# Two-layer decoder with a 32-expert MoE: the last expert pair's rows joined by one-hot products, the loop for crowded experts ahead of that pair

## The chip, the cores and the metric

One Trainium2 chip, and the program runs on one of its cores. The metric is device microseconds of one execution. Instructions run in order on each engine: PE (TensorE), DVE (VectorE), ACT (ScalarE), POOL (GpSimd) and SP (SyncE), which here only issues DMA and evaluates branches. An engine waits on semaphores that other engines or DMA transfers raise.

## The reference

`x` is 512 tokens of 1,024 features, and there are DEPTH = 2 layers, L0 and L1 here. Each layer mixes tokens (three kinds of attention behind one input projection `w_in`), takes a first layer norm, then a mixture of 32 experts with two experts per token, and a second layer norm:

```python
for l in range(DEPTH):
    mix = hybrid_mixer(x, tabs, w_in[l], ...)
    x = layer_norm(DEEPNORM_ALPHA * x + mix, ln1_g[l], ln1_b[l])
    moe = hier_moe(x, ...)
    x = layer_norm(DEEPNORM_ALPHA * x + moe, ln2_g[l], ln2_b[l])
return x
# in hier_moe: gate is zero but for the two experts of each token
h = jax.nn.silu(einsum('td,edf->tef', t, w_gate[g])) * einsum('td,edf->tef', t, w_up[g])
y = y + einsum('tef,efd->td', h * gate[:, g, :, None], w_down[g])
```

All values are float32.

## The kernel before, in words

**Expert stage.** An expert gets room for 64 token rows. Two experts fill the two halves of PE's array and make a *pair*; `p` runs over 16 pairs, pair 15 being the last. For a pair, GpSimd gathers its 128 rows from DRAM (`gathered`, L996), PE turns them (`turned`, L1007), `experts_up` multiplies by gate and up weights (32 products `S<-w,xg`), `experts_mid` takes SiLU (ACT L1040) and the product (DVE L1041), and `experts_down` transposes (PE L297), copies `hT` (ACT L90 and DVE L92 by turns) and multiplies by the down weights (16 products `o<-w,hT`). Two DVE instructions (L1055) scale the result and add it to the row's own share, in a row room of the tile `xroom`. A GpSimd DMA (L1056) then *scatter-adds* the 128 rows into the DRAM tensor `y2`, by the token index `ri`. So the sum over a token's experts is made in DRAM.

`load_next` (L530) issues the expert weights on SP's queue, as rooms of a ring come free. The last pair's weights are cut into smaller transfers.

**Crowded experts.** `overflow()` handles experts with more than 64 rows. Their number of extra *pieces* (`n_items`) is read from the chip's own counts, and a `tc.For_i` loop runs over them: each loads one expert's weights (two transfers, L1152), makes a list of rows, gathers them (L996), computes, and scatter-adds (L1218). With this data there are no pieces in L0 and one in L1: 33 gathers L996, 32 scatters L1056 and one scatter L1218 are in the profile. Where the loop is skipped or left, all engines meet: the branch on SP waits for every DMA queue lane used (DMASW0 to 7 are GpSimd's, DMAHW0 to 7 those of SP) and for the engines' sequencers.

**Second norm.** After the loop, `y2` is read back (L1263) as four tiles of 128 tokens (`yts`, the first in two halves). For each tile: statistics (DVE `bn_stats` L1272, `bn_aggr` L234), a power on POOL (L236), and scale and shift on DVE (L1275, L1277). In L1 the tile goes to the output. In L0 it is kept in DRAM (`res_dram`) and turned by PE (L1287, eight 128x128 transposes per tile), and each result is split into a rounded part `hi` (ACT, L210) and the rest `lo` (DVE, L213) of the next layer's input `xh`.

**Next projection.** The input projection of L1 (`acc<-U,xh`, and the same into banks `S` and `o`) multiplies `xh` by weight chunks: chunk 0 is 328 columns wide, the others 384. A chunk takes 24 products per token tile. Each weight chunk is loaded in four quarters (`load_pair`, L194), each with one cast for `hi` on ACT (L196) and one subtraction for `lo` (L199), on DVE and POOL by turns ("VG"). `warm(10)` issues ten products on constants behind the loop in L0.

`tc.issue_after(x)` places the following instructions behind `x` in its engine's program order; otherwise a scheduler orders instructions ahead of time.

Of the kernel before, what the change touches and what calls it, by code (L numbers as in the profile page):

```python
# [7 lines left out]
F32 = mybir.dt.float32  # L8
# [4 lines left out]
OP = mybir.AluOpType  # L13
# [51 lines left out]
def trunk(tc, a, out, dbg=None):  # L65
# [4 lines left out]
    with es:  # L70
# [9 lines left out]
        def bank(tag):  # L80
            return ps.tile([128, 512], F32, name=tag, tag=tag)
# [166 lines left out]
        for l in range(DEPTH):  # L248
# [739 lines left out]
            def row_room():  # L988
                turns["y"] += 1
                return carve(xroom, UNIT + 2 * D + D * (turns["y"] % 3), [D])  # L990
# [25 lines left out]
            def half_rows(xr, n=128):  # L1016

                y = row_room()
                V.tensor_tensor(y[0:n], xr[0:n], gb1[0:n, 0], OP.mult)
                V.tensor_tensor(y[0:n], y[0:n], gb1[0:n, 1], OP.add)  # L1020
                return y

            def next_half(p1):
                if p1 in XR:
                    with tc.issue_after(last_on["h"].ins):
                        HR[p1] = half_rows(XR.pop(p1))
                    fetch(p1 + 2)

            halves_ = ((0, 64), (64, 128))
# [13 lines left out]

            def experts_down(h, w, rows, y, p1):
                hT = cp.tile([128, 2, 128], F32, name="hT", tag="rw")
                transposes(hT.rearrange("p a b -> p (a b)"), [h[:, 0:128], h[:, 128:256]], 128)
                next_half(p1)
                o = [bank("o") for _ in range(2)]
                for f in range(2):
                    for n in range(2):  # L1050
                        for j, (c0, c1) in enumerate(halves_):
                            last_on["PE"] = mm(o[n][c0:c1], hT[:, f, c0:c1], down(w[j], f, n), f == 0, f == 1)
                for n in range(2):
                    c = slice(512 * n, 512 * n + 512)
                    last_on["V"] = V.scalar_tensor_tensor(y[:, c], o[n], rows[1], y[:, c], op0=OP.mult, op1=OP.add)  # L1055
                return G.indirect_dma_start(out=y2, out_offset=bass.IndirectOffsetOnAxis(ap=rows[0], axis=0), in_=y,  # L1056
                                            in_offset=None, bounds_check=S - 1, oob_is_err=False, compute_op=OP.add)

# [9 lines left out]
            def lists(b, P=None):  # L1068

                Pf = (P or hots(b)).rearrange("p t e s -> p t (e s)")  # L1070
                for q in range(2):
                    t = bank("T")
                    e0 = 4 * b + 2 * q
                    for i in range(NT):
                        mm(t[:, 0:6], Pf[:, i, 128 * q:128 * q + 128], tok[:, i, :, e0:e0 + 2], i == 0, i == NT - 1)
                    rv = small.tile([128, 3], F32, name="rv", tag="rv", bufs=8)
                    V.tensor_copy(rv[0:64], t[0:64, 0:6:2])
                    V.tensor_copy(rv[64:128], t[64:128, 1:6:2])
                    RI[2 * b + q] = slot_rows(rv)

            def fetch(p):
                if p < NE // 2:
# [62 lines left out]
            def overflow():  # L1145

                n_items = nc.values_load(eidi[0:1, MAX_ITEMS:MAX_ITEMS + 1], min_val=0, max_val=MAX_ITEMS)
                with tc.For_i(0, n_items) as item:
# [63 lines left out]
                    for f in range(2):  # L1212
                        for h, c in enumerate(two):
# [4 lines left out]
                    G.indirect_dma_start(out=y2, out_offset=bass.IndirectOffsetOnAxis(ap=ri[0:64], axis=0), in_=y[0:64], in_offset=None,  # L1218
                                         bounds_check=S - 1, oob_is_err=False, compute_op=OP.add)

            for p in range(NE // 2):
                w = (EW.pop(2 * p), EW.pop(2 * p + 1))
                gu = experts_up(XG.pop(p), w)
                load_next()
                h = experts_mid(gu)
                if p + 1 < NE // 2:
                    with tc.issue_after(last_on["up"].ins):
                        XG[p + 1] = turned(XR[p + 1])
                if p % 2 == 0 and p // 2 + 2 < NE // 4:
                    lists(p // 2 + 2)  # L1230
                st = experts_down(h, w, RI.pop(p), HR.pop(p), p + 1)
                load_next()
                if p % 2:
                    tc.declare_no_dep(st.ins, st0.ins, reason="a token has one group: the two pairs of a batch share no row")
                st0 = st
                if p == 3:
                    pieces()

            last = l == DEPTH - 1
            yus = [unit("A", "yt") for _ in range(2)]  # L1240
            gb2 = [yu[:, 2 * D:3 * D] for yu in yus]
            for j in range(2):
                SP.dma_start(gb2[j], a["ln_rows"][l:l + 1, 1, j].to_broadcast([128, D]))
# [12 lines left out]
            yts = []  # L1256
            for j in range(2):
                yu = carve(yus[j], 0, [2, D])
                for i in range(2):
                    yts.append(yu[:, i])  # L1260
                    r = 256 * j + 128 * i
                    for c in halves if r == 0 else [slice(0, 1024)]:
                        y2d = SP.dma_start(yu[:, i, c], y2[r:r + 128, c])  # L1263
            if not last:
                with tc.issue_after(y2d.ins):
                    Wc[l + 1, 1] = load_pair(w_in_src(l + 1, 1), chunks[1][1], "VG")
            for i in range(NT):
                z = yts[i]
                src = [z[:, c] for c in halves]
                st = small.tile([128, 2, 6], F32, name="bst", tag="bst", bufs=4)  # L1270
                for h in range(2):
                    V.bn_stats(st[:, h], src[h])  # L1272
# [10 lines left out]
                for h in range(2):  # L1283
                    t = bank("T")
                    for j in range(4):
                        k = 4 * h + j
                        PE.transpose(t[:, 128 * j:128 * j + 128], z[:, 128 * k:128 * k + 128], ident)  # L1287
                    split(*(XH[l + 1][:, r, 4 * h:4 * h + 4, 128 * i:128 * i + 128] for r in range(2)),
                          t.rearrange("p (k n) -> p k n", k=4))
            moe.__exit__(None, None, None)  # L1290


# [62 lines left out]
```

## Time and profile before

| | us |
|---|---|
| median of 3 runs | 1366.55 (1362.19, 1366.55, 1367.04) |
| profiled execution | 1363.18 |
| its span, first to last instruction | 1361.4 |
| PE busy | 1183.1 (87%) |
| DVE busy | 776.5 (57%) |
| ACT busy | 425.6 (31%) |
| POOL busy | 299.1 (22%) |
| mean granted TensorE clock | 0.953 of full speed |
| DMA | 293.82 MB, 216 GB/s over the span |

Times in the rows are microseconds from the span's start. The expert stages take about the stretches 500 to 645 (L0) and 1160 to 1335 (L1) of it. The profiled execution is 3.4 us (0.25%) under the median of the runs.

### The profile page before, as it was taken

How to read it: one execution, taken by the hardware profiler on the slowest of the kernel's cores; microseconds unless marked ns; L12 is line 12 of the kernel's file. 1: busy time of each engine (PE TensorE's matmuls, PEld its weight loads, DVE VectorE, ACT ScalarE, POOL GpSimd, SP SyncE). 2: the span in 40 equal slices, each digit the busy share in tenths (PEclk: the TensorE clock that was granted, in tenths of full speed). 3: DMA queues.
4: the chain of work that ended last, by engine and by line, in shares of the span. 5: the costliest groups of instructions: out<-in, count | busy, mean ns of one | idle time of the engine just before them, and what ended most of it. 6: DMA issues, size and time to landing. Idle time of an engine off the chain costs nothing. (4 is left out here: it accounts for less than half of the span.)

```text
span 1361.4 us, 18270 instructions
## 1 busy us (share of the span) xinstructions
PE 1183.1 (87%) x6708; PEld 822.5 (60%) x6708; DVE 776.5 (57%) x1905; ACT 425.6 (31%) x1019; POOL 299.1 (22%) x288
## 2 busy tenths in 40 slices
PE   6989999999969997778599899999998799887850
PEld 6989986668944443333398899666797343333320
DVE  6599638674455654323668992667636465433435
ACT  3362257574111111110236322857711111111100
POOL 5332431300011211110342434230010122111101
PEclk9999999999979999999799999899999899998975
DMA  6341340005298999998552424200336899999943
GB/s 233 116 147 57 124 170 12 28 10 216 77 377 330 406 406 411 412 382 298 186 160 77 133 75 140 98 24 23 138 126 246 316 395 408 407 409 409 349 178 125
DMA packets 65115, 293.82 MB, mean 216 GB/s; under 512 B 16000, under 2 KB 20608, under 8 KB 49664
## 3 DMA queue, kind: packets, MB, share of 16 engines
q1 hardware_dynamic: 54496, 271.63, 51.9%
q0 software_dynamic: 9376, 16.81, 5.1%
q10 hardware_dynamic: 1152, 4.19, 0.8%
q8 instruction: 54, 0.88, 0.2%
q14 instruction: 37, 0.30, 0.1%
HBM read 278.06 MB, written 31.82 MB: 228 GB/s over the span
## 5 line engine op out<-in xcount | busy, mean ns | idle before, releaser
L97 PE MATMUL acc<-U,xh 128*128 128x384 f32 (+1 forms) x1584 | 294.8, 339 | 20.5 <-DVE xh L212 7.2
L97 PE MATMUL S<-w,xg 128*64 128x512 f32 (+1 forms) x968 | 270.4, 607 | 45.2 <-DMA w<-w_e 31.2
L97 PEld LDWEIGHTS acc<-U,xh 128*128 128x128 f32 x1584 | 275.3, 190 | 24.6 <-ACT U L196 7.2
L97 PEld LDWEIGHTS S<-w,xg 128*64 128x64 f32 x968 | 91.5, 141 | 171.2 <-issue 100.3
L97 PE MATMUL o<-w,hT 128*64 128x512 f32 x488 | 134.2, 615 | 7.5 <-ACT hT L90 3.9
L1040 ACT ACTIVATE h<-S 128x256 f32<-128x256 f32 x32 | 12.3, 384 | 377.7 <-PE S L97 377.7
L199 POOL TENSOR_TENSOR U<-raw,U 128x768 fp32r<-128x768 f32 (+2 forms) x46 | 90.5, 1972 | 164.5 <-ACT U L196 164.4
L1041 DVE TENSOR_TENSOR h<-h,S 128x256 f32<-128x256 f32 x32 | 13.5, 421 | 189.4 <-ACT h L1040 189.4
L996 POOL DMA_INDIRECT xroom<-xd,ri x33 | 40.6, 1230 | 275.6 <-issue 142.7
L196 ACT ACTIVATE U<-raw 128x768 fp32r<-128x768 f32 (+2 forms) x88 | 68.1, 812 | 85.7 <-PE acc L97 42.1
L1056 POOL DMA_INDIRECT y<-xroom,ri x32 | 51.0, 1595 | 177.2 <-DVE xroom L1055 158.9
L97 PEld LDWEIGHTS o<-w,hT 128*64 128x64 f32 x488 | 43.6, 140 | 73.9 <-issue 51.0
L1055 DVE SCALAR_TENSOR_TENSOR xroom<-o,rv,xroom 128x512 f32<-128x512 f32 x64 | 48.0, 750 | 56.3 <-PE o L97 52.3
L199 DVE TENSOR_TENSOR U<-raw,U 128x768 fp32r<-128x768 f32 (+2 forms) x42 | 51.9, 1238 | 39.5 <-ACT U L196 36.9
L1011 ACT ACTIVATE xg<-acc,lv 128x128 f32<-128x128 f32 x128 | 48.2, 456 | 58.7 <-PE acc L1007 57.5
L90 ACT ACTIVATE uc<-T 128x512 f32<-128x512 f32 (+3 forms) x117 | 51.5, 461 | 40.8 <-PE T L297 39.0
L97 PE MATMUL acc<-U,oh 128*128 128x384 f32 (+1 forms) x384 | 63.3, 315 | 0.0
L97 PEld LDWEIGHTS acc<-U,oh 128*128 128x128 f32 x384 | 56.8, 189 | 1.3 <-issue 1.0
L1007 PEld LDWEIGHTS acc<-cst,xroom 128*128 128x128 f32 x256 | 30.5, 152 | 41.9 <-issue 27.4
L403 DVE MATCH_REPLACE8 uc<-m,uc 128x256 f32<-128x256 f32 (+2 forms) x96 | 51.3, 539 | 0.0
L1013 DVE TENSOR_SCALAR xg<-acc,lv 128x128 f32<-128x128 f32 x128 | 43.6, 402 | 13.5 <-PE acc L1007 13.4
L1007 PE MATMUL acc<-cst,xroom 128*128 128x128 f32 x256 | 38.6, 299 | 14.3 <-DMA xroom<-xd,ri 14.3
(366 smaller groups left out, 1991.7 us busy)
## 6 DMA issues: line engine op xcount, KB each, us to landing
w<-w_e SPq DMA_DIRECT2D x110, 1536.0 KB, 30.7
raw<-w_in SPq DMA_DIRECT2D x64, 384.0 KB, 3.6
xroom<-w_e SPq DMA_DIRECT2D x8, 1536.0 KB, 28.3
w<-w_e SPq DMA_DIRECT2D x24, 512.0 KB, 17.3
raw<-w_o SPq DMA_DIRECT2D x16, 384.0 KB, 3.6
y<-uc SPq DMA_DIRECT2D x2, 2048.0 KB, 7.8
xd<-yn ACTq DMA_DIRECT2D x8, 512.0 KB, 6.8
xroom<-w_e SPq DMA_DIRECT2D x4, 768.0 KB, 14.6
```

Of the source, the lines that this page charges most:

```text
L90: A.activation(o, i, AF.Copy, scale=1.0 if scale is None else scale)
L97: return PE.matmul(o, l, r, start=start, stop=stop, skip_group_check=True)
L196: A.activation(hi, r, AF.Copy)
L199: e.tensor_tensor(lo, r, hi.bitcast(F32), OP.subtract)
L403: V.match_replace(out=acc_t[i][:, :n], in_to_replace=m8, in_values=acc_t[i][:, :n], imm_value=TAKEN)
L996: G.indirect_dma_start(out=xr[0:n], out_offset=None, in_=xd, in_offset=bass.IndirectOffsetOnAxis(ap=ri[0:n], axis=0), bounds_check=S - 1, ...
L1007: PE.transpose(t[:, 128 * j:128 * j + 128], xr[:, 128 * k:128 * k + 128], ident)
L1011: A.activation(xg[:, k], o, AF.Identity, scale=lv[:, 0, k, 0:1], bias=lv[:, 0, k, 1:2])
L1013: V.tensor_scalar(xg[:, k], o, lv[:, 0, k, 0:1], lv[:, 0, k, 1:2], op0=OP.mult, op1=OP.add)
L1041: last_on["h"] = V.tensor_tensor(h, h, gu[:, FH:2 * FH], OP.mult)
L1055: last_on["V"] = V.scalar_tensor_tensor(y[:, c], o[n], rows[1], y[:, c], op0=OP.mult, op1=OP.add)
L1056: return G.indirect_dma_start(out=y2, out_offset=bass.IndirectOffsetOnAxis(ap=rows[0], axis=0), in_=y, in_offset=None, bounds_check=S - 1, ...
```

## The change

Five things are changed.

1. In the last pair, the 128 rows stay in an SBUF tile `y_last` and aren't scattered. `pT`, four transposes of that pair's one-hot lists, turns slots back into tokens: eight products `pT`^T x `y_last` (two 512-wide halves for each of the four tiles) give each token tile's share in PSUM. In L0 DVE adds it to the tile read back (L1295, eight additions). In L1 PE also multiplies the tile read back by the identity into the same PSUM bank, and the norm reads PSUM.
2. A new function `sums()`, called at pair 15 ahead of its `experts_up`, holds `overflow()` and then the loads of `ln_rows` and of the four `y2` tiles, the first no longer in two halves.
3. Chunk 0 of the next projection is loaded within the last `experts_down`, with all four `lo` subtractions on DVE ("V"). Chunk 1 is loaded after the norm of tile 0.
4. `hT` is always copied on DVE.
5. `warm(10)` is left out.

```diff
@@ experts_down
-                transposes(hT.rearrange("p a b -> p (a b)"), [h[:, 0:128], h[:, 128:256]], 128)
+                transposes(hT.rearrange("p a b -> p (a b)"), [h[:, 0:128], h[:, 128:256]], 128, None, "V")
                 next_half(p1)
+                if w_next:
+                    w_next.pop()()
...
+                return y
+
+            def added(y, rows):
                 return G.indirect_dma_start(out=y2, out_offset=bass.IndirectOffsetOnAxis(ap=rows[0], axis=0), in_=y,
                                             in_offset=None, bounds_check=S - 1, oob_is_err=False, compute_op=OP.add)
...
+            def next_weights():
+                with tc.issue_after(last_on["h"].ins):
+                    Wc[l + 1, 0] = load_pair(w_in_src(l + 1, 0), chunks[0][1], "V")
+
+            def sums():
+
+                overflow()
+                yus = [unit("A", "yt") for _ in range(2)]
+                for j in range(2):
+                    SP.dma_start(yus[j][:, 2 * D:3 * D], a["ln_rows"][l:l + 1, 1, j].to_broadcast([128, D]))
+                for j in range(2):
+                    yu = carve(yus[j], 0, [2, D])
+                    for i in range(2):
+                        yts.append(yu[:, i])
+                        r = 256 * j + 128 * i
+                        y2d = SP.dma_start(yu[:, i], y2[r:r + 128, :])
+                return [yu[:, 2 * D:3 * D] for yu in yus], y2d
+
             for p in range(NE // 2):
                 w = (EW.pop(2 * p), EW.pop(2 * p + 1))
+                if p == PL:
+                    gb2, y2d = sums()
                 gu = experts_up(XG.pop(p), w)
...
+                y = experts_down(h, w, rows, HR.pop(p), p + 1)
                 load_next()
...
+                if p < PL:
+                    st = added(y, rows)
...
-            with tc.issue_after(last_on["PE"].ins), tc.issue_after(last_on["V"].ins), tc.issue_after(st.ins):
-                if not last:
-                    raw_room()
-                    Wc[l + 1, 0] = load_pair(w_in_src(l + 1, 0), chunks[0][1], "VG")
-            overflow()
...
-                warm(10)
...
+            for i in range(NT):
+                zb[i] = [bank(("acc", "S", "o")[i % 3]) for _ in halves]
+                for t, c in zip(zb[i], halves):
+                    if last:
+                        mm(t, ident, yts[i][:, c], True, False)
+                    mm(t, pT[:, i], y_last[:, c], not last, True)
             for i in range(NT):
                 z = yts[i]
-                src = [z[:, c] for c in halves]
+                src = [z[:, c] for c in halves] if not last else zb[i]
+                if not last:
+                    for t, c in zip(zb[i], halves):
+                        V.tensor_tensor(z[:, c], z[:, c], t, OP.add)
```

**SP's queue, end of L0's expert stage.** L530 are expert weights, L1243 the norm's `ln_rows`, L194 quarters of chunk 0, and L1147 to L1148 the loop's branch; the last row is where all engines meet. Before:

```order
L530 DMA w<-w_e 128x1024 [waits DMAHW3_49]
L1243 DMA yt<-ln_rows 128x1024 [waits DMAHW4_49,PE_49]
L1243 DMA yt<-ln_rows 128x1024 [waits DMAHW5_49,PE_49]
L194 DMA raw<-w_in 128x656 [waits DMAHW6_49,PE_49]
L194 DMA raw<-w_in 128x656 [waits DMAHW7_49]
L194 DMA raw<-w_in 128x656 [waits DMAHW0_49]
L194 DMA raw<-w_in 128x656 [waits DMAHW1_49]
L1147 TENSOR_LOAD eidi [waits DVE_49]
L1148 COMPARE_AND_BRANCH
L1148 UNCONDITIONAL_BRANCH [waits SP_sequencer_49,DMAHW2_49,DMAHW3_49]
L1148 UNCONDITIONAL_BRANCH [waits DMASW4_49,DMASW3_49,DMASW5_49,DMASW2_49,DMASW6_49,DMASW1_49,DMASW7_49,DMASW0_49,DMAHW0_49,SP_sequencer_49,DMAHW1_49,DVE_sequencer_49,DMAHW2_49,PE_sequencer_49,DMAHW3_49,Activation_sequencer_49,DMAHW4_49
```

The same place in the change (the branch is L1153 to L1154 there):

```order
L530 DMA w<-w_e 128x1024 [waits DMAHW0_49]
L530 DMA w<-w_e 128x1024 [waits DMAHW1_49]
L530 DMA w<-w_e 128x1024 [waits DMAHW2_49]
L530 DMA w<-w_e 128x1024 [waits DMAHW3_49]
L1153 TENSOR_LOAD eidi [waits DVE_49]
L1154 COMPARE_AND_BRANCH
L1154 UNCONDITIONAL_BRANCH [waits SP_sequencer_49,DMAHW4_49,DMAHW5_49]
L1154 UNCONDITIONAL_BRANCH [waits DMASW4_49,DMASW3_49,DMASW5_49,DMASW2_49,DMASW6_49,DMASW1_49,DMASW7_49,DMASW0_49,DMAHW0_49,SP_sequencer_49,DMAHW1_49,DVE_sequencer_49,DMAHW2_49,PE_sequencer_49,DMAHW3_49,Activation_sequencer_49,DMAHW4_49
L1380 BRANCH_PREFETCH_HINT
```

The meeting place now follows the last expert weights directly, and `ln_rows`, the `y2` reads and chunk 0 stand behind it. On PE the 48 products of pair 15 stand behind it too.

**PE, L0, behind the expert stage.** One piece of the difference: transposes of the norm's tiles (L1287 before, L1313 now) and products of the next projection (`U,xh`), whose banks are `acc` for tile 0, `o` for tile 1, `S` for tile 2 and `acc` again for tile 3. The last rows are tile 3's last four transposes of the change. Behind them it has 21 and 24 products left of tile 1's chunks 0 and 1; before, tile 3's last four transposes have only the last 8 products of tile 1's chunk 1 behind them. Then follow tile 2's 48 and tile 3's 48 in both.

```order
+L1313 MATMUL T<-cst,yt 128x128 x16
 L97 MATMUL acc<-U,xh 128x328 x24
-L97 MATMUL acc<-U,xh 128x384 x18
-L1287 MATMUL T<-cst,yt 128x128 x8
-L97 MATMUL acc<-U,xh 128x384 x6
+L97 MATMUL acc<-U,xh 128x384 x3
+L1313 MATMUL T<-cst,yt 128x128 x8
+L97 MATMUL acc<-U,xh 128x384 x21
+L97 MATMUL o<-U,xh 128x328
+L1313 MATMUL T<-cst,yt 128x128 x4
+L97 MATMUL o<-U,xh 128x328 x2
+L1313 MATMUL T<-cst,yt 128x128 x4
```

The transposes of the later tiles have moved ahead of most products of the tiles before them.

**DVE, L0, from the last pair into the norm of tile 0.** L92 copies `hT`, L199 are the `lo` subtractions (656 wide: chunk 0, 768 wide: chunk 1), L1057 is the scale-and-add of the last pair. In the change:

```order
L92 COPY hT<-T 128x256
L199 TENSOR_TENSOR U<-raw,U 128x656
L1057 SCALAR_TENSOR_TENSOR y_last<-o,rv,y_last 128x512
L199 TENSOR_TENSOR U<-raw,U 128x656 x2
L1057 SCALAR_TENSOR_TENSOR y_last<-o,rv,y_last 128x512
L199 TENSOR_TENSOR U<-raw,U 128x656
L1295 TENSOR_TENSOR yt<-yt,acc 128x512
L199 TENSOR_TENSOR U<-raw,U 128x768
L1295 TENSOR_TENSOR yt<-yt,acc 128x512
L1298 BN_STATS bst<-yt 128x6 x2
L199 TENSOR_TENSOR U<-raw,U 128x768
L234 BN_AGGR mv<-bst 128x2
```

Before, two of chunk 0's four subtractions are POOL's, and one stands between the meeting place and the first statistics; in the change all four, and one of chunk 1, stand ahead of the statistics.

## Rows read from the trace of the kernel before

**Rows 1.** Windows: window, length, PE, PEld, DVE, ACT, POOL, clock, DMA share, GB/s.

```profile
1240.00:1270.00 30.00, 26.13 (x106) 8.96 (x106) 8.66 (x14) 2.61 (x8) 4.98 (x4) 0.94 0.99 392
656.50:668.00 11.50, 6.89 (x20) 3.41 (x20) 8.35 (x14) 2.26 (x4) 4.99 (x4) 0.50 0.88 320
740.00:800.00 60.00, 56.53 (x324) 54.79 (x323) 57.00 (x143) 24.07 (x55) 19.85 (x22) 0.97 0.31 96
```

**Rows 2.** Timeline of L0's end, all engines: start, us, instruction, [idle before <-releaser].

```profile
633.86 1.55 POOL L1056 DMA_INDIRECT y<-xroom,ri  x1 [11.10 <-DVE xroom L1055]
...
648.62 1.55 POOL L1056 DMA_INDIRECT y<-xroom,ri  x1 [13.21 <-DVE xroom L1055]
...
649.66 0.84 DVE L199 TENSOR_TENSOR U<-raw,U 128x656 fp32r<-128x656 f32 x1 [1.50 <-ACT U L196]
...
656.34 1.39 ACT L196 ACTIVATE U<-raw 128x656 fp32r<-128x656 f32 x2 [6.03 <-DMA y<-xroom,ri]
...
656.76 4.45 PE L97 MATMUL o<-bfc 128*128 128x512 bf16 x10 [9.39 <-DVE ctr L1143]
...
659.66 0.69 DVE L1272 BATCH_NORM_STATS2 bst<-yt 128x6 f32<-128x512 f32 x1 [0.63 <-DMA yt<-y]
```

**Rows 3.** Timeline of SP's queue, end of L0.

```profile
631.64 0.33 SPq L530 DMA_DIRECT2D w<-w_e  x1
...
656.89 2.46 SPq L1263 DMA_DIRECT2D yt<-y  x5
```

**Rows 4.** DMA issues in 631:633, 633:636, 648:650: size, us to landing.

```profile
w<-w_e SPq DMA_DIRECT2D x1, 512.0 KB, 13.7
...
y<-xroom,ri POOLq DMA_INDIRECT x1, 8.7
...
y<-xroom,ri POOLq DMA_INDIRECT x1, 6.8
```

**Rows 5.** Timeline, the expert pairs: early in L1, then its last ones.

```profile
1065.55 8.40 PE L97 MATMUL S<-w,xg 128*64 128x512 f32 x32
...
1278.02 7.08 PE L97 MATMUL S<-w,xg 128*64 128x512 f32 x30
...
1290.51 1.61 DVE L1055 SCALAR_TENSOR_TENSOR xroom<-o,rv,xroom 128x512 f32<-128x512 f32 x2 [0.53 <-PE o L97]
```

**Rows 6.** DVE groups by shape, 656 to 692: busy, mean ns | idle before.

```profile
L213 DVE TENSOR_TENSOR xh<-T,xh 128x512 fp32r<-128x512 f32 x8 | 5.3, 688 | 0.2 <-ACT xh L210 0.2
L1272 DVE BATCH_NORM_STATS2 bst<-yt 128x6 f32<-128x512 f32 x8 | 5.3, 674 | 2.1 <-DMA yt<-y 2.1
L199 DVE TENSOR_TENSOR U<-raw,U 128x768 fp32r<-128x768 f32 x2 | 2.9, 1453 | 0.0
```

**Rows 7.** Timeline, L0: first transposes, last norm, last transposes, last tile's products.

```profile
665.56 1.97 PE L1287 MATMUL T<-cst,yt 128*128 128x128 f32 x8 [4.36 <-DVE yt L1277]
...
686.41 1.41 DVE L1277 SCALAR_TENSOR_TENSOR yt<-yt,mv 128x512 f32<-128x512 f32 x2
...
687.96 0.63 PE L1287 MATMUL T<-cst,yt 128*128 128x128 f32 x4
...
689.82 7.94 PE L97 MATMUL S<-U,xh 128*128 128x328 f32 x48
```

**Rows 8.** Timeline of L1's loop and second norm.

```profile
1297.20 0.96 SPq L1152 DMA_DIRECT2D w<-w_e  x2
...
1306.90 0.23 DVE L1155 TENSOR_SCALAR h<-cst,ctr 128x16 f32<-128x16 f32 x1
...
1312.38 1.00 POOL L996 DMA_INDIRECT xroom<-xd,ri  x1 [3.72 <-DVE ri L982]
...
1319.14 6.17 PE L97 MATMUL S<-w,xg 128*64 128x256 f32 x32 [2.51 <-DVE xg L1198]
...
1330.74 1.44 POOL L1218 DMA_INDIRECT y<-xroom,ri  x1 [17.35 <-DVE xroom L1217]
...
1335.04 2.51 SPq L1263 DMA_DIRECT2D yt<-y  x5
...
1340.38 0.69 DVE L1272 BATCH_NORM_STATS2 bst<-yt 128x6 f32<-128x512 f32 x1 [1.33 <-DMA yt<-y]
```

**Rows 9.** Last lines of two source views: weights L1152, gathers L996.

```profile
DMA to landing us min/median/max: 13.1/15.2/17.3
...
DMA to landing us min/median/max: 3.1/9.7/12.9
```

More of the change, by code (lines that the diff above doesn't have):

```diff
@@ L1014, in turned, with half_rows @@
                 return xg
-            def half_rows(xr, n=128):
-                y = row_room()
+            def half_rows(xr, n=128, y=None):
+                y = row_room() if y is None else y
                 V.tensor_tensor(y[0:n], xr[0:n], gb1[0:n, 0], OP.mult)
@@ L1025, in next_half @@
                     with tc.issue_after(last_on["h"].ins):
-                        HR[p1] = half_rows(XR.pop(p1))
+                        HR[p1] = half_rows(XR.pop(p1), y=y_last if p1 == NE // 2 - 1 else None)
                     fetch(p1 + 2)
@@ L1079, in lists @@
                     RI[2 * b + q] = slot_rows(rv)
+                return Pf
             def fetch(p):
@@ L1219, in overflow @@
                                          bounds_check=S - 1, oob_is_err=False, compute_op=OP.add)
+            last, PL, w_next, yts = l == DEPTH - 1, NE // 2 - 1, [], []
+            pT = mo.tile([128, NT, 128], F32, name="pT", tag="pT")
+            y_last = mo.tile([128, D], F32, name="y_last", tag="y_last")
+            def next_weights():
[13 more added lines that the diff above has]
+                return [yu[:, 2 * D:3 * D] for yu in yus], y2d
             for p in range(NE // 2):
                 w = (EW.pop(2 * p), EW.pop(2 * p + 1))
+                if p == PL:
+                    gb2, y2d = sums()
                 gu = experts_up(XG.pop(p), w)
@@ L1225, in trunk @@
                 h = experts_mid(gu)
-                if p + 1 < NE // 2:
+                if p < PL:
                     with tc.issue_after(last_on["up"].ins):
                         XG[p + 1] = turned(XR[p + 1])
+                elif not last:
+                    raw_room()
+                    w_next.append(next_weights)
                 if p % 2 == 0 and p // 2 + 2 < NE // 4:
-                    lists(p // 2 + 2)
-                st = experts_down(h, w, RI.pop(p), HR.pop(p), p + 1)
-                load_next()
-                if p % 2:
-                    tc.declare_no_dep(st.ins, st0.ins, reason="a token has one group: the two pairs of a batch share no row")
-                st0 = st
+                    Pf = lists(p // 2 + 2)
+                    if p // 2 + 2 == NE // 4 - 1:
+                        transposes(pT.rearrange("p a b -> p (a b)"), [Pf[:, i, 128:256].bitcast(F32) for i in range(NT)], 128)
+                rows = RI.pop(p)
+                y = experts_down(h, w, rows, HR.pop(p), p + 1)
+                load_next()
+                if p < PL:
+                    st = added(y, rows)
+                    if p % 2:
+                        tc.declare_no_dep(st.ins, st0.ins, reason="a token has one group: the two pairs of a batch share no row")
+                    st0 = st
                 if p == 3:
                     pieces()
[L1239 to L1243, printed above, removed]
-            with tc.issue_after(last_on["PE"].ins), tc.issue_after(last_on["V"].ins), tc.issue_after(st.ins):
-                if not last:
-                    raw_room()
-                    Wc[l + 1, 0] = load_pair(w_in_src(l + 1, 0), chunks[0][1], "VG")
-            overflow()
             if not last:
-                warm(10)
                 XH[l + 1] = xhp.tile([128, 2, NK, S], F32R, name="xh", tag="xh")
@@ L1255, in trunk @@
             halves = [slice(0, 512), slice(512, 1024)]
[L1256 to L1266, printed above, removed]
+            zb = {}
+            for i in range(NT):
[4 more added lines that the diff above has]
+                    mm(t, pT[:, i], y_last[:, c], not last, True)
             for i in range(NT):
                 z = yts[i]
-                src = [z[:, c] for c in halves]
+                src = [z[:, c] for c in halves] if not last else zb[i]
+                if not last:
+                    for t, c in zip(zb[i], halves):
+                        V.tensor_tensor(z[:, c], z[:, c], t, OP.add)
                 st = small.tile([128, 2, 6], F32, name="bst", tag="bst", bufs=4)
@@ L1289, in trunk @@
                           t.rearrange("p (k n) -> p k n", k=4))
+                if i == 0:
+                    with tc.issue_after(y2d.ins):
+                        Wc[l + 1, 1] = load_pair(w_in_src(l + 1, 1), chunks[1][1], "VG")
             moe.__exit__(None, None, None)
```

## Prediction

> **What bounds the kernel now.** I read the windows first, to see what each stage is short of. Late in an expert stage the DMA engines are busy 0.99 of the time at 392 GB/s, while PE has 26.13 of 30 us and DVE 8.66 [rows 1]: the stage lasts as long as its weights take. In L1's projections and attention PE works 56.53 and DVE 57.00 of 60 us [rows 1]: what comes late there stays late. Between the two lies the stretch that the change rebuilds, so I read its timeline, engine by engine, in both layers.
>
> In L0 the last expert weights are issued at 631.64 [rows 3] and take 13.7 to land [rows 4], so they are there at 645.3. Pair 15 runs while they come in, and its scatter is issued at 648.62 [rows 2]. The scatter takes 6.8 [rows 4], to 655.4, and everything stands until then: ACT idles 6.03 "<-DMA y" [rows 2], and PE comes out of the meeting place at 656.76, 1.3 us after the landing. Then `y2` is read (656.89 [rows 3]), the first statistics start at 659.66 [rows 2], and the norm of tile 3 ends at 686.41 + 1.41 = 687.82 [rows 7].
>
> In L1 pair 14 ends at 1290.51 + 1.61 = 1292.12 [rows 5], pair 15 ends before 1306.90, the one piece runs from 1306.90 to its scatter at 1330.74, `y2` is read from 1335.04, and the statistics of tile 0's second half start at 1340.38 [rows 8].
>
> **The change in L0.** It removes pair 15's scatter and the read behind it from the path: from 648.6 to 659.66, some 11 us. It pays by moving the meeting place ahead of pair 15, and that is where the sum turns.
>
> (a) The branch waits for SP's DMA lanes. Ahead of it stand pair 15's weights, which land at 645.3; pair 14's scatter, 633.86 [rows 2] + 8.7 [rows 4] = 642.6, is earlier. With the 1.3 us seen above, PE starts pair 15 at 646.6. Before, most of pair 15 was done by then; now none is.
>
> (b) A pair takes 1292.12 − 1278.02 = 14.1 us [rows 5]. That row has PE at speed (30 of the 32 products recorded, 7.08). A pair behind an idle stretch needed 8.40 [rows 5]; PE will have idled since pair 14, whose scatter is issued at 633.86 [rows 2], some 13 us, so I add 1.3. The bounds are 0 and 2.6: L1's piece, also after idling, took 6.17 for 32 products of half the width, 2.6 over half of 7.08 [rows 8]. Pair 15 then ends at 662.0.
>
> (c) Of chunk 0's subtractions on DVE, two stand between the last two scale-and-adds (2 x 0.84 [rows 2] = 1.7). One follows, then an addition (0.69 as an L213 of the same shape [rows 6]), one subtraction of chunk 1 (0.98, 0.84 scaled by 768/656), and the other addition: 3.2. The products of `y_last`, 0.47 each as an estimate (two half-width products at 7.08/30), hide behind the subtraction. The first statistics start at 662.0 + 1.7 + 3.2 = 666.9, **7.2 later** than 659.66. If the subtractions fall into waits, as one did at 649.66 [rows 2], 3.5 of it goes; at the 1453 ns that two took beside POOL [rows 6] it is some 2.5 more.
>
> (d) From the first statistics to tile 3's end were 28.2 us. The 2.1 us waiting for `y2` go [rows 6]; of 2.9 for two L199 [rows 6] about 1.0 stays; six more additions cost 4.1: +0.1. So tile 3 is 7.3 late.
>
> (e) PE's order. Behind tile 3's last transposes stood 80 products up to the end of its chunk 0 (8 + 48 + 24); now 117 (21 + 24 + 48 + 24). In 689.82's row 48 take 7.94 [rows 7], 0.165 each, and before, they followed the transposes at 687.96 at once. The 37 that PE could have done while it waited for DVE now come after: **+6.1**. It would be 0 if PE reached that place late anyway.
>
> L0 together: **+13.4**, bounds +2.5 (no clock loss, subtractions hidden, order free) and +17.2.
>
> Without a price: the `hT` copies on DVE and the four transposes of `pT` lie under the weights' transfer [rows 1]; without that cover each is under a microsecond a pair. `ln_rows`, `y2` and chunk 0, now issued behind the meeting place, are about 4.3 MB, 11 us at 392 GB/s [rows 1], and land by 658, under pair 15.
>
> **warm(10).** Its ten products took 4.45 [rows 2], and the clock was 0.50 (1.2 GHz) from 656.5 to 668 all the same [rows 1]; the first eight transposes took 1.97 behind them, against 0.63 for four later [rows 7]. So I price the removal at 0.
> The Trainium skill, page "TensorE: Matmul & The Clock Gate", section "Part 1: The HAM clock gate (the "warmup" mystery)", says that the array is at half clock by default and that sustained work releases it. By that rule pair 15's 48 products, now right ahead of the norm, could do what the ten did not: the first transposes would take 1.3 in place of 1.97, and the sum would be 0.7 lower.
>
> **The change in L1.** Here the piece has to run either way; the order is turned around.
>
> (f) The piece begins at 1292.12, and its gather is issued 5.48 later, as before (1312.38 − 1306.90), at 1297.6. Before, the queues were empty by then and it landed in 3.1, the minimum; the median gather, among streaming weights, takes 9.7 [rows 9], and pair 15's weights are still coming. I take 9.7: 1307.3, and the products 3.7 later (1319.14 less 1312.38 + 3.1), at 1311.0. The piece's weights were issued at 1297.20 [rows 8] and landed 13.1 and 17.3 later [rows 9], the first at 1310.3; without 1 MB of `ln_rows` ahead of them (2.6 us at 392 GB/s), 1307.7. They don't bind.
>
> (g) From products to scatter 11.6, from there to the read 4.3 [rows 8]: pair 15 starts at 1326.9. Add 14.1, 1.3 for the clock, 0.9 for identity products that stand between its own, 0.7 for the first product and the first half's statistics: the second half's start at 1343.9, against 1340.38. **+3.5**. With the gather at 3.1 the weights bind, +0.2; at 12.9, +6.7.
>
> **Sum.** 1363.18 + 13.4 + 3.5 = **1380 us**, bounds 1366 and 1387. The sum stands on the profiled execution, 3.4 us under the median of the runs, a quarter of a per cent.
>
> **Rivals.**
> *A. The meeting place does not hold pair 15* (not slower). If the engines pass the skipped loop in L0 without waiting for the weights, pair 15 ends at 648.6 as now. (c) then makes it 653.5 with its 4.9, 6.2 ahead of 659.66; with (d) and (e) L0 is even, and L1's 3.5 gives 1367; with (e) at 0, 1361. It decides once pair 15 ends some 7 us ahead of (b)'s 662.0: then the sum falls within half a per cent of before. For it: only one branch of a skipped loop is taken. Against it: the branch names all DMASW and DMAHW lanes, and the same branch held ACT 6.03 us for a scatter [rows 2]. Chance 0.16.
> *B. L0's delay is made up in L1's attention.* Then only L1's 3.5 stays: 1367. For it: the norm may not be on the path of what comes later, a loaded DVE. Against it: from 740 to 800 PE lacks 3.5 us of 60, DVE 3.0 [rows 1], so 13 us find no room. Half made up gives 1373. Chance 0.17.
> *C. The forecast*, both layers later. Chance 0.67.
>
> **How the numbers follow.** A difference of 0.5%, 6.8 us, is about what a measurement of this kernel tells from none: 1359.7 to 1373.4. C is slower throughout but for its lowest corner (0.03). Of A, 0.09 is faster, where (e) is free and L1's gather quick, the rest the same. Of B, 0.13 is the same and 0.03 slower; 0.01 faster. So faster 0.10, same 0.23, slower 0.67. The range runs from A's 1361 to C's upper bound of 1387 with the 3.4 us of the median added: 1361 to 1391. C alone would be 1368 to 1391.
>
> **What would show it.** (a): in L0 the first `S<-w,xg` of pair 15 near 646.6, with all engines released together after the last weights; before 640 is rival A. (b): pair 15 some 15.4 long, its first products slower than its later ones. (c): first statistics near 667, no idle DVE ahead of them. (d), (e): tile 3's last transposes near 695, and its chunk 0 done near 715 instead of 701. (f): the piece's gather landing some 10 us after its issue. (g): the second statistics of L1 about 17 us later than now in absolute time. The forecast is wrong if PE starts pair 15 early, if PE is still busy when tile 3's transposes come (no 6.1), or if the stretch behind 740 shows idle time that takes the delay up.

## The result, and the profile after the change

The change makes the kernel slower: 1376.3 us (median of 6 runs, 1372.0 to 1378.3) against 1364.8 before (6 runs, 1361.6 to 1368.3), a ratio of 1.0079 with a 95% interval of 1.0056 to 1.0102. The profiled execution took 1375.41, its span is 1373.6, 12.2 longer than that of before.

Of these 12.2 us, 2.9 don't belong to the change. They arise in the first 128 us of the span, where both kernels issue the same instructions in the same order (ACT's runs 0.3 late at 56 us, 1.5 at 80, 2.9 from 128 on). The other kernels profiled below are 1.4 to 4.2 late there too: the profile of before happened to be a quick one. "Net" below means less a kernel's own lateness there, 2.9 for the change. Net, the change's span is 9.3 longer; the medians differ by 11.5.

The first view is L0's last pair, from the timelines of all engines of the changed kernel:

```profile
623.57 12.63 SPq L530 DMA_DIRECT2D w<-w_e  x7
...
637.03 1.55 POOL L1061 DMA_INDIRECT y<-xroom,ri  x1 [11.51 <-DVEq L1154]
...
650.52 1.11 PE L97 MATMUL S<-xroom,xg 128*64 128x512 f32 x1 [14.60 <-DVE ctr L1149]
...
651.64 2.45 SPq L1246 DMA_DIRECT2D yt<-y  x4
...
654.80 0.59 PE L97 MATMUL S<-xroom,xg 128*64 128x512 f32 x1
...
666.60 0.74 DVE L1057 SCALAR_TENSOR_TENSOR y_last<-o,rv,y_last 128x512 f32<-128x512 f32 x1
...
669.48 0.68 DVE L1295 TENSOR_TENSOR yt<-yt,acc 128x512 f32<-128x512 f32 x1
670.08 1.28 DVE L1298 BATCH_NORM_STATS2 bst<-yt 128x6 f32<-128x512 f32 x2
```

PE stands for 14.60 us and starts pair 15 only when the meeting place opens, 14.3 us after the last weights were issued (636.2), close to the forecast's 13.7 + 1.3. The first statistics come at 670.08 against 659.66 [rows 2], 7.5 later net. The windows show the stand, the slow start (clock 0.53) and, in the last row, the norm:

```profile
636.80:650.50 13.70, 0.00 (x0) 0.00 (x0) 0.04 (x1) 0.00 (x0) 1.68 (x2) 0.66 0.38 109
650.50:655.00 4.50, 4.48 (x12) 1.38 (x14) 0.02 (x1) 0.00 (x0) 0.16 (x1) 0.53 0.70 208
655.00:667.40 12.40, 10.94 (x45) 3.58 (x42) 4.65 (x8) 3.64 (x6) 0.00 (x0) 1.00 0.90 333
...
675.40:699.40 24.00, 14.19 (x73) 13.54 (x73) 21.29 (x42) 5.83 (x8) 3.22 (x6) 0.65 0.41 153
```

In the norm PE works 14.19 of 24 us. Its own timeline shows at what it waits:

```profile
677.49 1.97 PE L1313 MATMUL T<-cst,yt 128*128 128x128 f32 x8 [5.12 <-DVE yt L1303]
687.18 1.94 PE L1313 MATMUL T<-cst,yt 128*128 128x128 f32 x8 [7.72 <-DVE yt L1303]
688.77 5.98 PE L97 MATMUL acc<-U,xh 128*128 128x328 f32 x27
...
700.66 0.60 PE L1313 MATMUL T<-cst,yt 128*128 128x128 f32 x4
...
716.23 8.98 PE L97 MATMUL acc<-U,xh 128*128 128x328 f32 x54
```

Between the transposes of tiles 0 and 1 PE idles 7.72 us. Tile 3's last transposes are 9.8 late net (687.96 in [rows 7]), and its chunk 0 starts at 716.23 against 697.60, 15.7 late net.

L1, pair 14's end (1302.23) to the first norm, from the timelines:

```profile
1302.30 0.23 DVE L1161 TENSOR_SCALAR h<-cst,ctr 128x16 f32<-128x16 f32 x1
...
1307.69 1.00 POOL L996 DMA_INDIRECT xroom<-xd,ri  x1 [3.62 <-DVE ri L982]
...
1315.13 1.22 DVE L1019 TENSOR_TENSOR xroom<-xroom,gb 64x1024 f32<-64x1024 f32 x1 [8.24 <-DMA xroom<-xd,ri]
...
1330.30 1.44 POOL L1224 DMA_INDIRECT y<-xroom,ri  x1 [21.61 <-DVE xroom L1223]
...
1334.97 1.11 PE L97 MATMUL S<-xroom,xg 128*64 128x512 f32 x1 [6.51 <-issue]
...
1354.34 0.70 DVE L1298 BATCH_NORM_STATS2 bst<-acc 128x6 f32<-128x512 f32 x1 [0.16 <-PE acc L97]
```

The piece starts right behind pair 14, its gather takes 7.4 us, pair 15 follows the meeting place at 1334.97. From pair 14's end to these statistics are 52.1 us; before it was 48.3 [rows 5, 8].

### The profile page after: what moved, and what is told of

It reads as the page before. It is cut to its first block, busy times and chain, and to the rows that moved or that the text cites. A ratio compares the mean times of both kernels' runs of the same rounds, so it can differ in the third digit from the quotient of the medians.

```text
span 1373.6 us, 18378 instructions
## 1 busy us (share of the span) xinstructions
PE 1206.6 (88%) x6754; PEld 830.2 (60%) x6754; DVE 789.9 (58%) x1930; ACT 422.4 (31%) x1006; POOL 296.1 (22%) x284
## 4 chain that ended last, share of the span: by engine, by line
PE 51%; DMA 25%; DVE 6%; issue 4%; ACT 2%; POOL 1%; SPq 0%; DVEq 0%; ACTq 0%; POOLq 0%
PE acc L97 23%; DMA w<-w_e 22%; PE S L97 12%; PE o L97 10%; PE T L297 5%; DMA xroom<-xd,ri 1%; PE acc L1007 1%; DMA y<-xroom,ri 1%; ACT uc L90 1%; DMA yt<-y 1%; DVE yt L1303 0%; DVE yt L1301 0%; DVE U L199 0%; PE T L1313 0%; PE T L97 0%
## 5 line engine op out<-in xcount | busy, mean ns | idle before, releaser
L97 PE MATMUL acc<-U,xh 128*128 128x384 f32 (+1 forms) x1584 | 298.4, 342 | 16.6 <-DVE xh L212 7.3
L97 PE MATMUL S<-w,xg 128*64 128x512 f32 (+1 forms) x968 | 275.7, 613 | 36.7 <-DMA w<-w_e 20.3
L97 PEld LDWEIGHTS acc<-U,xh 128*128 128x128 f32 x1584 | 280.1, 193 | 18.8 <-issue 7.2
L97 PE MATMUL o<-w,hT 128*64 128x512 f32 x488 | 130.1, 610 | 8.8 <-DVE hT L92 7.9
L199 POOL TENSOR_TENSOR U<-raw,U 128x768 fp32r<-128x768 f32 (+2 forms) x44 | 89.3, 2034 | 190.3 <-ACT U L196 170.0
L996 POOL DMA_INDIRECT xroom<-xd,ri x33 | 44.2, 1340 | 273.6 <-issue 163.8
L97 PEld LDWEIGHTS o<-w,hT 128*64 128x64 f32 x488 | 40.0, 139 | 77.2 <-issue 58.2
L1061 POOL DMA_INDIRECT y<-xroom,ri x30 | 47.6, 1588 | 147.0 <-DVE xroom L1057 127.6
L199 DVE TENSOR_TENSOR U<-raw,U 128x768 fp32r<-128x768 f32 (+2 forms) x44 | 53.5, 1220 | 35.7 <-ACT U L196 32.8
L97 PE MATMUL S<-xroom,xg 128*64 128x512 f32 x88 | 47.9, 689 | 27.4 <-DVE ctr L1149 14.6
L1057 DVE SCALAR_TENSOR_TENSOR xroom<-o,rv,xroom 128x512 f32<-128x512 f32 x60 | 45.0, 750 | 39.8 <-PE o L97 36.4
```

Source lines behind the costliest of these rows:

```text
L97: return PE.matmul(o, l, r, start=start, stop=stop, skip_group_check=True)
L199: e.tensor_tensor(lo, r, hi.bitcast(F32), OP.subtract)
L996: G.indirect_dma_start(out=xr[0:n], out_offset=None, in_=xd, in_offset=bass.IndirectOffsetOnAxis(ap=ri[0:n], axis=0), bounds_check=S - 1, ...
```

## The experiments

Theory 1 is that of the prediction: the meeting place holds pair 15 in L0, PE's order costs 6, and L1 only some 3.5. The rivals are that the added work costs the time, or that L1 does, and that L1's attention takes up delays whatever they are. Each time is a median and a ratio to the kernel before on the same chip, with its 95% interval; 1% is 13.7 us. Runs of one kernel differ by several us, so a difference of 2 or 3 us between two medians is not shown unless the intervals part.

**no_loop_L0.** The change without the loop in L0 (no pieces there, nothing left undone).

```diff
-                overflow()
+                if last:
+                    overflow()
```

> The change, with the loop for crowded experts left out in L0 alone (it has no pieces there with this data, so nothing is left undone). Theory 1, the meeting place holds pair 15: without it pair 15 runs while its weights land, as before the change, and L0's first statistics come some 13 us earlier than in the change, ahead of those of before; half to all of it reaches the end: 1362 to 1370 us against 1376. Theory 2, the delay comes from the added work (subtractions, additions, products) and the place of the loop matters little: the first statistics move by under 3 us and the time stays within 3 us of 1376.

1372.4, ratio 1.0045 (1.0031 to 1.0058). The first statistics start here:

```profile
655.77 1.28 DVE L1299 BATCH_NORM_STATS2 bst<-yt 128x6 f32<-128x512 f32 x2
...
675.81 1.94 PE L1314 MATMUL T<-cst,yt 128*128 128x128 f32 x8 [13.47 <-DVE yt L1304]
```

That is 14.3 earlier than in the change (both executions were 2.7 to 2.9 late at the start): the meeting place is what held pair 15, theory 1. But the time fell by 4, and theory 1 had expected 6 to 14. One part of the rest is seen in the second row: PE's wait ahead of tile 1 has grown to 13.47. The other part came to light with the last run.

**loop_ahead.** Before, with the loop alone moved.

```diff
                 w = (EW.pop(2 * p), EW.pop(2 * p + 1))
+                if p == NE // 2 - 1:
+                    overflow()
...
-            overflow()
```

> The kernel before, with only the loop moved ahead of pair 15: scatter, read back, chunk 0 and norm are as before. Theory 1: in both layers pair 15 runs behind the meeting place and its scatter and the read back behind it, so L0's first statistics come 12 to 13 us later than before and L1's 13 to 14: 1383 to 1391 us against 1365. Theory 2: no worse than the change itself, 1365 to 1376.

1388.1, ratio 1.0155 (1.0130 to 1.0181): 22 us slower, as theory 1 had it.

```profile
651.13 1.12 PE L97 MATMUL S<-xroom,xg 128*64 128x512 f32 x1 [14.97 <-DVE ctr L1143]
...
665.50 1.64 DVE L1055 SCALAR_TENSOR_TENSOR xroom<-o,rv,xroom 128x512 f32<-128x512 f32 x2 [3.81 <-PE o L97]
...
676.77 0.69 DVE L1273 BATCH_NORM_STATS2 bst<-yt 128x6 f32<-128x512 f32 x1 [3.34 <-DMA yt<-y]
```

The same stand of 15 us, and behind it the scatter and the read back. The loop's place alone is worse than the change; what the rows on chip save is part of the difference, and the order of copies shown under parity another.

**banks.** The change, one name in a tuple: tile 3's one-hot products go to bank S.

```diff
-                zb[i] = [bank(("acc", "S", "o")[i % 3]) for _ in halves]
+                zb[i] = [bank(("acc", "S", "o", "S")[i]) for _ in halves]
```

> The change, with the one-hot products of tile 3 in bank S in place of acc. Theory 1: tile 3's products hold the acc banks until DVE's additions of tile 3, and the next projection, whose first tile wants acc, waits for them; that is why the transposes stand ahead of the products. With S the first products run between the norms of tiles 0 and 1, tile 3's chunk 0 is done some 6 us earlier, and 2 to 6 us of it reach the end: 1370 to 1374. Theory 2: the order costs nothing since PE is late anyway: within 1 us of 1376.

1372.6, ratio 1.0044 (1.0031 to 1.0057), 3.7 less than the change at the median. PE's timeline:

```profile
677.03 1.97 PE L1313 MATMUL T<-cst,yt 128*128 128x128 f32 x8 [2.36 <-DVE yt L1303]
678.83 0.91 PE L97 MATMUL acc<-U,xh 128*128 128x328 f32 x2
...
688.07 1.04 PE L1313 MATMUL T<-cst,yt 128*128 128x128 f32 x8
```

The projection's first products start at 678.83 and not at 688.77, and fill the gap ahead of tile 1's transposes. So the order of the change was not a whim of the scheduler: tile 3's one-hot products held `acc` until DVE's additions of tile 3. In the change these read:

```profile
687.56 0.67 DVE L1295 TENSOR_TENSOR yt<-yt,acc 128x512 f32<-128x512 f32 x1
688.26 0.63 DVE L1295 TENSOR_TENSOR yt<-yt,acc 128x512 f32<-128x512 f32 x1
```

and `acc<-U,xh` follows at 688.77.

**loop_behind.** The change, with `sums()` called behind the loop over the pairs, so that the loop and the read back follow pair 15.

```diff
-                if p == PL:
-                    gb2, y2d = sums()
...
+            gb2, y2d = sums()
```

> The change, with the loop and the read back behind pair 15 again; the rows of pair 15 still stay on chip. Theory 1: in L0 all engines meet as soon as pair 15 is done, since there is no scatter of its rows to wait for, and the first statistics come 5 us ahead of those of before and 12 ahead of the change; L1 is as before within 2 us: 1361 to 1368. Theory 2, the one-hot products and additions cost what the scatter did: not under 1372.

1368.7, ratio 1.0016 (1.0005 to 1.0028): 7.6 us less than the change, a little above what was expected. The first statistics (661.66, and 3.2 late at the start) came 8.7 ahead of the change, net, and only 1.2 ahead of before, where 12 and 5 were expected. In both layers `ln_rows` now stood ahead of the read back.

**behind_ln.** As loop_behind, `ln_rows` ahead of the loop.

```diff
             def sums():
-                overflow()
                 yus = [unit("A", "yt") for _ in range(2)]
...
+                overflow()
```

> The change with the loop and the read back behind pair 15, as in the run loop_behind (1368.7), but with the loads of ln_rows ahead of the loop again. Theory 1: behind the meeting place the read back stood in SP's queue and in the DMA engines behind 1 MB of ln_rows, in both layers; ahead of the loop that megabyte is hidden, the first statistics come some 3 us earlier in L0 and 3 to 5 in L1: 1360 to 1366. Theory 2: the read back of y2 is what takes the time, and ln_rows beside it costs nothing: within 1.5 us of 1368.7.

1366.7, ratio 1.0013 (0.9997 to 1.0029). 2 us less at the median, but with ratios that differ by 0.0003: not told apart from loop_behind. It lies between the two theories, and where `ln_rows` stands was not shown to matter.

**behind_ln_banks.** As behind_ln, with bank S, and tile 0 read in halves.

```diff
+                        for c in (slice(0, 512), slice(512, 1024)) if r == 0 else [slice(0, 1024)]:
+                            y2d = SP.dma_start(yu[:, i, c], y2[r:r + 128, c])
```

> As behind_ln, with the one-hot products of tile 3 in bank S (as in the run banks) and tile 0 read back in halves as before the change. Theory 1: the gains of the three add, since they lie one after the other: 1356 to 1363, ahead of both kernels. Theory 2: L1's attention takes up what L0 gains, as it took up part of the change's delay: 1363 or more, no faster than before.

1360.4, ratio 0.9964 (0.9950 to 0.9979): faster than both kernels, for a reason that parity below puts in doubt. Even here the engines meet late in L0:

```profile
651.39 1.61 DVE L1057 SCALAR_TENSOR_TENSOR y_last<-o,rv,y_last 128x512 f32<-128x512 f32 x2 [4.79 <-PE o L97]
656.91 0.29 POOL L1109 CAST tok<-cst 128x128 fp32r<-128x128 f32 x1 [17.58 <-DVEq L1154]
657.40 2.96 SPq L1247 DMA_DIRECT2D yt<-y  x5
...
660.74 0.69 DVE L1295 TENSOR_TENSOR yt<-yt,acc 128x512 f32<-128x512 f32 x1 [2.94 <-DMA yt<-y]
```

Pair 15 is done at 653.0, and the engines part at 656.9, 3.9 later: DVE has chunk 0's four subtractions to do first (3.09 from 652.91). The next two runs test this.

**late_V** and **late_VG.** As behind_ln_banks, with chunk 0 loaded behind the read back, its subtractions on DVE, or on DVE and POOL by turns.

```diff
-                    w_next.append(next_weights)
...
             gb2, y2d = sums()
+            if not last:
+                next_weights()
```

> As behind_ln_banks, with chunk 0's loads and subtractions (all on DVE) behind the loop and the read back. Theory 1: in behind_ln_banks the engines meet some 3 us late in L0, since chunk 0's transfers stand behind ln_rows and DVE subtracts ahead of the meeting place; behind it the meeting comes 3 us earlier, of which 0 to 2 are left, as the subtractions now lie in the norm: 1358 to 1361. Theory 2: DVE bounds that stretch wherever the subtractions stand: 1360 to 1364.

> As late_V, with the subtractions by turns on DVE and POOL. Theory 1: two of four leave DVE, which bounds the norm: 1 to 2 us faster than late_V, 1357 to 1360. Theory 2: beside POOL's subtractions DVE's instructions take twice as long, as 1.91 against 0.84 before the change: no faster than late_V.

1364.3, ratio 0.9987 (0.9967 to 1.0007), and 1360.0, ratio 0.9959 (0.9942 to 0.9976). The engines now part 0.5 after pair 15 is done (650.89 after 650.36, and 654.02 after 653.49), so chunk 0's transfers, casts and subtractions were what held the meeting. But moving them into the norm gains nothing at the end: DVE has to do them somewhere. Giving two to POOL there wins back 4 us at the median, with intervals that overlap a little (0.9967 to 0.9976).

**vg.** The change, chunk 0's subtractions on DVE and POOL by turns, as before it: `chunks[0][1], "V"` becomes `"VG"`.

> The change, with chunk 0's subtractions on DVE and POOL by turns, as before. Theory 1: two subtractions of 0.84 leave DVE's path between pair 15 and the first statistics, which come 1 to 2 us earlier; 1373 to 1376. Theory 2: POOL's two run beside DVE's and make both slower (1.9 and more in place of 0.84), and POOL's is what the next projection then waits for: no gain, 1376 to 1379.

1376.5, ratio 1.0088 (1.0065 to 1.0111): no gain. The first statistics came 1.6 earlier net than in the change, as theory 1 had it, but nothing of it is left at tile 3's last transposes (702.03 and 700.66, the same net). In the norm of tile 0, which took 8.5 up to its transposes and not 7.4, DVE's instructions beside POOL's subtractions (here chunk 1's) were longer, much as theory 2 had it: L199 2.39 and L1301 2.22, in the change 1.62 and 1.55. So handing two subtractions to POOL does not make the change faster; what they cost on DVE by themselves was not shown.

**warm_ahead.** The change, with 54 products on constants ahead of the loop in L0.

```diff
                 if p == PL:
+                    if not last:
+                        warm(54)
                     gb2, y2d = sums()
```

> The change, with 54 products on constants put ahead of the loop in L0, where PE only waits for the last weights. Theory 1: pair 15's first five steps took 0.85 us each in place of 0.43 because PE had idled 14 us; with PE kept busy they take 0.43, and the first statistics come 2 us earlier: 1373 to 1375. Theory 2: the steps are slow for another reason (weights just landed, the meeting place), and nothing moves: 1376.

1378.9, ratio 1.0092 (1.0071 to 1.0112). On the time, a miss. PE's timeline:

```profile
638.15 11.81 PE L97 MATMUL o<-bfc 128*128 128x512 bf16 x52
652.12 0.64 PE L97 MATMUL S<-xroom,xg 128*64 128x512 f32 x1 [2.16 <-POOL tok L1109]
...
652.60 0.59 PE L97 MATMUL S<-xroom,xg 128*64 128x512 f32 x1
```

The cause of the slow steps is confirmed: with PE busy up to 2.2 us ahead, the granted clock is 1.00 from the first one on (0.53 in the change), and they are 0.59 long and 0.43 apart, where the change has 1.06 and 0.85. But the 2 us don't arrive at the end. In this execution the last weights were issued 1.5 later net than in the change, pair 15 started 1.9 later, and the first statistics came only 0.1 earlier. Then the norm of tile 0 took 9.2 up to its transposes and not 7.4:

```profile
675.71 0.15 DVE L237 TENSOR_SCALAR mv<-mv 128x1 f32<-128x1 f32 x1 [2.49 <-POOL mv L236]
675.78 2.35 DVE L1303 SCALAR_TENSOR_TENSOR yt<-yt,mv 128x512 f32<-128x512 f32 x1
```

DVE waited 2.49 for POOL's power, which stood behind one of chunk 1's subtractions on POOL, and its next instruction took 2.35 beside the other. That is one profiled execution; whether the other three lost the 2 us in the same way isn't known.

**ahead_L1.** As behind_ln_banks, with L1 as in the change: the loop ahead of pair 15.

```diff
+                if last and p == PL:
+                    gb2, y2d = sums()
...
-            gb2, y2d = sums()
+            if not last:
+                gb2, y2d = sums()
```

> As behind_ln_banks (1360.4), but in L1 alone the loop stands ahead of pair 15, as in the change. Theory 1, the term of the prediction for L1: the piece has to run on either side, so the move costs only what its gather loses among streaming weights and pair 15 loses at half clock, 1 to 4 us: 1361 to 1365. Theory 2: the change's delay is mostly L1's: 1367 or more.

1360.1, ratio 0.9965 (0.9946 to 0.9984), the same as behind_ln_banks. In L1 the loop's place costs nothing that can be measured, with intervals that would hide some 3 us; the change's loss is mostly L0's.

**parity.** Neither theory explains why L1's attention took up 7 us of the change's delay and none of no_loop_L0's. Copies of transposes out of PSUM go to ACT and DVE by turns of one counter. Each layer of the kernel before makes an odd number of such copies in its expert stage (16 `hT` and one in the loop); the change adds one for `pT`, and no_loop_L0 drops the loop's again. So L1's copies change engine with the change, and back with no_loop_L0. One of them, in L1's attention, is `qk<-T`. In the kernel before it is ACT's, and its turn comes behind 2.17 us of casts (L591); DVE waits 5.93 for products of the copied tile, and ACT 2.82 for DVE:

```profile
857.54 2.17 ACT L591 ACTIVATE q<-ua 64x1024 fp32r<-64x1024 f32 x2
859.73 0.60 ACT L90 ACTIVATE qk<-T 128x512 f32<-128x512 f32 x1
862.42 0.69 DVE L569 TENSOR_REDUCE stC<-S 128x4 f32<-128x512 f32 x1 [5.93 <-PE S L97]
863.15 1.14 ACT L572 ACTIVATE dp<-S,stC 128x128 f32<-128x128 f32 x4 [2.82 <-DVE stC L569]
```

In the change the copy is DVE's. The kernel before, with the counter moved on by one, has ACT's order of the change there:

```diff
+            turn["t"] += 1
             moe.__exit__(None, None, None)
```

> The kernel before, with one edit that computes nothing: the counter by which PSUM copies go to ACT and DVE by turns is moved on by one at the end of L0, as the change moves it by its pT copy. Theory 1: in the change L1's attention gave back most of what it gave back because the turned copies put ACT's instructions in another order there, in which PE no longer waits 2.45 us and then runs at half clock: the stall is gone here too, and the time falls by 2 to 6 us, to 1360 to 1364. Theory 2: attention took up the delay because it has slack, whatever the order: the stall stays, or goes without a gain, and the time is that of before within 1.5 us.

1358.7, ratio 0.9948 (0.9929 to 0.9967): 7.5 us faster than before by an edit that computes nothing, a little more than expected. The same rows in the run parity, which runs 3.2 later than before at this place:

```profile
859.60 0.68 DVE L92 COPY qk<-T 128x512 f32<-128x512 f32 x1
861.39 0.69 DVE L569 TENSOR_REDUCE stC<-S 128x4 f32<-128x512 f32 x1 [1.11 <-PE S L97]
862.93 1.14 ACT L572 ACTIVATE dp<-S,stC 128x128 f32<-128x128 f32 x4
```

DVE makes the copy before ACT has begun its casts (860.73), 3.3 us earlier once the 3.2 are taken off, and behind them ACT goes on without a wait. The same ACT line L572 is what PE then waits for. Windows and PE's wait in the kernel before:

```profile
862.00:870.00 8.00, 6.67 (x51) 5.16 (x48) 7.37 (x12) 6.80 (x23) 1.94 (x2) 1.00 0.00 0
870.00:880.00 10.00, 8.09 (x38) 5.95 (x39) 7.46 (x21) 7.58 (x34) 1.92 (x1) 0.66 0.09 8
```

```profile
871.76 0.79 PE L97 MATMUL S<-k,q 128*128 128x256 f32 x2 [2.45 <-ACT dp L572]
```

The same stretch in parity, and then in the change:

```profile
863.00:873.00 10.00, 9.41 (x66) 7.37 (x65) 8.19 (x15) 9.21 (x33) 5.40 (x3) 1.00 0.00 2
```

```profile
884.00:894.00 10.00, 9.25 (x61) 6.36 (x60) 8.86 (x29) 9.13 (x38) 2.35 (x1) 1.00 0.08 7
```

In the kernels whose copies fall as before (before, no_loop_L0, loop_ahead) PE waits 2.45 us for ACT at this place; in the change, in parity and in all nine others it waits 0.58 or 0.59. In before the clock is then 0.66 for 10 us, in the change and in parity it stays at 1.00. Between 850 and 890 us parity gains 4.7 us on the kernel before, and the change's delay shrinks by 4.3. The other 2.8 of parity's shorter span come from L1's last pairs on, and why was not followed; so the wait in attention accounts for some 4.7 of the 7.5.

## Why the prediction was right

It forecast slower, 1380 with 1361 to 1391, and 1376.3 was measured; the direction and the place are confirmed, and most terms by their size. That the number came so near is in part luck: the two layers' terms came out at 19.6 net where 16.9 was forecast, and some 10 of it was made up at places where the sum had nothing: 8.5 in L1 ahead of its last pair, 1.7 in its norm.

- **(a)** The meeting place holds pair 15: PE started at 650.52, 647.6 net, where 646.6 was forecast. Shown by no_loop_L0, where the first statistics come 14.3 earlier. Rival A, that the skipped loop holds nothing, is out.
- **(b)** The slow start is there: five steps at 0.85 in place of 0.43, 2.1 where 1.3 was forecast. Pair 15 with its two subtractions took 16.8 (17.1 forecast).
- **(c)** First statistics 7.5 late net, 7.2 forecast. vg takes two of the subtractions off DVE, and the time stays.
- **(d)** Too small: tile 3's transposes were 9.8 late net, so that the norm's stretch grew by 2.3 and not by 0.1. Between these points DVE was busy 25.23 us before and 27.56 now, 2.3 more, where the prediction's additions less subtractions make 2.2. What failed is the 2.1 that it took off for the wait for `y2`: that wait is gone, but DVE still idles 3.0 in all (3.1 before), 1.3 of it for ACT's L210 (0.2 before).
- **(e)** 15.7 less 9.8 is 5.9, forecast 6.1. The size was right, and the mechanism only half: the prediction called it PE's order, and the run banks shows that the order follows from a PSUM bank that DVE frees late. banks regained 3.7 at the end.
- **(f), (g)** The gather took 7.4, between 3.1 and 9.7; what it saved was used up behind the meeting place, by pair 15 and the identity products (19.4 from 1334.97 to 1354.34, 17.0 forecast). Together 3.9 against 3.5. The norm behind it was then 1.7 shorter (below), which the sum lacks. ahead_L1 confirms that L1's order is worth little either way.
- **warm(10)** at 0: the first transposes took 1.97 as before. PE had just worked, but then idled 5.12 ahead of them, and the granted clock from 677.4 to 679.4 was 0.50 (1.2 GHz). So the 0.7 that the prediction set beside its sum did not come. It had drawn it from the Trainium skill, page "TensorE: Matmul & The Clock Gate", section "Part 1: The HAM clock gate (the "warmup" mystery)", where half clock is the default and activity lifts it; the trace agrees with that, and what the prediction left out was the idle time between.
- **Rival B**, the delay made up in L1's attention, came half true: 15.7 net at 716 us, 9.0 at 1000, 7.2 when pair 14 ends in L1. But slack, the rival's reason, is not what took it up. In loop_ahead and no_loop_L0, whose copies fall as before, attention gave nothing back: 13.8 net at tile 3's chunk 0 and 14.1 at the products that before has at 1000, and 4.7 and 5.9. The step that failed is the one that set against it that PE lacks 3.5 us of 60 from 740 to 800. That window was full, but between 862 and 880 the kernel before had a wait and a half clock that the change's extra copy removes. The prediction looked for slack and not for a change of order; the moved `hT` and `pT` copies were priced at nothing by their duration alone. That stretch is 4.3 of the 6.7 that attention gave back; the other 2.4 fell off between 716 and 850, where parity gains 0.6, and were not followed.

So the parts that were priced cost more than the result shows. Taking the copies' order out, an estimate is 1.0079 / 0.9948 = 1.0132, some 18 us, if all of parity's gain applies to the change, and 11.5 + 4.3 = 15.8 by the part that the change's own trace shows; the sum has 16.9. By the same measure the best versions with the rows on chip, 0.9959 to 0.9965, are no faster than the kernel before with its counter moved, 0.9948: their intervals overlap, and a gain from keeping the rows on chip was not shown.

Left open: the 2.8 us of parity behind attention, the 2.4 of the change's delay that went before 850, and whether all runs of warm_ahead lost their 2 us as the profiled one did.

## What to carry to other kernels

A skipped loop is not free: its branch waits for every transfer issued ahead of it, so whatever is moved behind it loses its overlap with those transfers. Ask of PSUM results that are produced early which later user wants the same bank, and when the reader lets go of it. And where copies alternate between engines by a counter, an edit that adds or removes one copy changes the engine of all later ones: compare kernels with the counter at the same place before crediting the edit.

## What the runs showed of the hardware

POOL's power L236, one column, took 0.99 us in the second norms of before, and 0.55 in L1's of the change. The first row is POOL's timeline in L1 of before:

```profile
1347.35 0.99 POOL L236 TENSOR_TENSOR mv<-mv,mhalf 128x1 f32<-128x1 f32 x1 [4.76 <-DVE mv L235]
```

and these are POOL's in the change, L0's tiles 1 and 2 and one of L1:

```profile
683.41 0.99 POOL L236 TENSOR_TENSOR mv<-mv,mhalf 128x1 f32<-128x1 f32 x1 [7.49 <-DVE mv L235]
689.04 0.55 POOL L236 TENSOR_TENSOR mv<-mv,mhalf 128x1 f32<-128x1 f32 x1 [4.64 <-DVE mv L235]
...
1360.78 0.55 POOL L236 TENSOR_TENSOR mv<-mv,mhalf 128x1 f32<-128x1 f32 x1 [4.17 <-DVE mv L235]
```

In the slow cases DVE runs L1275 (L1301 in the change) beside it, with its inputs in SBUF; in the quick ones it runs the same operation reading PSUM, or at 689.04 an L213 that reads PSUM. Four times 0.44 is as much as the 1.7 us by which L1's norm became shorter. The Trainium skill, page "SBUF — State Buffer", section "Who interferes with whom", says that a VectorE instruction with two SBUF inputs contends with a GpSimd instruction that reads SBUF, and one with at most one SBUF input, outside its 2-port modes, does not; the trace agrees.
